# Layer 0's gate columns on TensorE in the scan, layer 1's mix columns behind layer 0's experts, longer runs in layer 1's experts, and the second mixer's norms by halves

## The chip, the core and the metric

The kernel runs on one core of one Trainium2 chip. A core has TensorE (PE, matrix products), VectorE (DVE), ScalarE (ACT), GpSimd (POOL) and SyncE (SP), each with its own queue of instructions that it executes in order, and 16 DMA engines that move data between the chip's large memory and the core's own. The metric is the device time of one execution, in microseconds (us).

## The reference, cut to what matters

One call runs two layers of one model and then a block of another on 512 latent tokens of width 1024 (layer 0 also on 256 context tokens):

```
for i in (0, 1):
    mod_l = split(silu(c) @ ada_w[i] + ada_b[i], 6)        # six vectors of 1024; mod_c alike from c_ctx
    h = rmsnorm(x, norm_mix_g[i]) * (1 + mod[1]) + mod[0]
    x = x + mod[2] * mixer_i(h)                            # mLSTM, then retention
    h = rmsnorm(x, norm_ffn_g[i]) * (1 + mod[4]) + mod[3]
    x = x + mod[5] * expert_choice_ffn(h)                  # 16 experts, each takes its top tokens
x = rmsnorm(x, final_norm_g)
hn = rms_norm(x, attn_norm_g_2); proj = hn @ w_in_2        # then attention, GLA, pooling, ffn
```

An expert computes silu(xs @ w_gate) * (xs @ w_up), times w_down, for its 64 latent (32 context) tokens; the results are added back to the tokens' rows with the gate as weight.

## The kernel before, in words

The stages follow each other on TensorE: norms and the qk dense of the mLSTM (to about 120 us), its v dense (to 208), its sigmoid gate dense (to 293), the scan (to 410), out-projection and routing (to 540), layer 0's experts (to 1101), retention (to 1404), out-projection and routing (to 1486), layer 1's experts (to 1964), and the second block with its mixer and ffn (to the end).

**Dense products** are exact splits: each fp32 matrix is a high and a low part (whi, wlo; hhi, hlo), and three matmuls (L295 to L297) make one product, a triple. Into these runs, `fill(n)` puts steps of waiting generators, n steps per triple: 2 means two steps after each triple, 0.25 one in four. What is left at a dense's end is emptied by `fill(1000)`.

**Modulation columns.** `ada_chunk` (L165 and around) computes one of the six vectors of a layer for both c and c_ctx: VectorE multiplies 1024 x 1024 weights by silu(c) into ada_v, 16 instructions, two for each of eight row blocks; TensorE sums over the partitions with 16 f32 matmuls in 32 records (L170); a gate vector (2, 5) goes to memory as `modd`, the others become columns. Chunks 2 to 5 of layer 0 are the generators of the sigmoid gate dense, each of six steps. `ada_mix` (L205 to L233) computes vectors 0 and 1 of layer 1 on TensorE instead: eight loads of 1 MB, 32 matmuls (64 records, L217), a copy on ScalarE (L221), four transposes, and three VectorE instructions. It is the generator of the scan, where `fill(2)` (L685) takes two steps at a time. The generator of the v dense is `mlstm_gates` (tiles pc, L541 to L583), 54 steps.

**Layer 0's experts.** `expert_stream` hands out a ring of 20 weight slots in a fixed order: four of the stream's own (w), wb0, ot, whb, whp, wb1. `st.get()` gives the next loaded slot, `st.done()` issues the load of the next chunk into the slot that has come free; a chunk is 1 MB, eight f32 records of 512 columns in the latent form (L879). TensorE's order is written out by hand (`pinned`). At the end of the last expert its two results are multiplied by the gates (yl, yc, L1157) and scattered into xl and xc by GpSimd (L1158); seven warming matmuls (L114) run on yl; all pools of the stage are closed; the retention loads its tokens from xl and xc into rt_x (L1524), norms them (L361), transposes them (L1533) and starts its first dense.

**Layer 1's experts** take 64 tokens each, and the groups of tokens lie ready for two experts at a time. Odd experts (and expert 0) *gather* for the next pair: eight gathers of eight records each (L1306; tile tp, three buffers), evicted by ScalarE and VectorE in turn (L1310, L1308) into xT, then `facts` (L1318). Two gathers lie ahead of the transposes of hl (L1392), two behind them, and one after each quarter of the down product (tile dl). Even experts add the results of the pair before: `combine` makes eight sums (tile cb, two buffers, L1345 and L1346), each followed by a VectorE addition into X (L1348). The first stands in the up product (tile pl) after its first quarter, then one per quarter, one behind it, two after hl = silu * up (L1385), two after the transposes. `split` (L1325 to L1331) prepares the results for the sums in two halves of 64 rows, b = 0 then 1; for odd experts (sw = 1) half b is put at place b ^ 1, and the sums read place 0 first. The last eight sums stand alone at the stage's end.

**Second mixer** (L1829 and on): for each of four token tiles, ScalarE squares and sums x (L1829), VectorE (tiles 0 and 3) or GpSimd (1 and 2) multiplies by the final norm's weight (L1830), ScalarE squares again (L1831), two reciprocal roots follow (`rstd`, L100 and L102; a root needs a table load on ScalarE when another function was there before), VectorE makes the normed tile (L1842), TensorE transposes it (L1770), and the first dense runs a tile behind (L295 to L297). For tile 0 TensorE is kept warm with small matmuls (L114) on the results of the chain.

## Time and profile before

| | us |
|---|---|
| median of 3 runs | 2591.66 (2591.22 to 2591.9) |
| the profiled execution | 2597.43 |
| its span | 2595.6 |
| TensorE busy in it | 2488.7 |
| VectorE busy | 1078.6 |
| ScalarE busy | 699.0 |
| GpSimd busy | 555.1 |
| mean granted clock of TensorE | 0.977 |

The span is the time between the first and the last recorded instruction. Busy is the time in which an engine works on an instruction; a matmul of TensorE appears as a row (PE) beside its weight load (PEld), and rows of one run overlap, so a run is measured from start to start. The granted clock is 1.0 at 2.4 GHz and 0.5 at 1.2 GHz. A row in order of time has its start, its duration, engine, line, operation, the written tile <- the read ones, their count, and in brackets the idle time before it with what ended it. SPq rows are issues of DMAs. A row of a stretch (window) has its start and end, its length, the busy us of PE, PEld, DVE, ACT and POOL with the instructions of each, the granted clock, the DMA engines' mean share and the GB/s that they moved.

### The profile page before, as it was taken

To read this page: it belongs to the slowest core of one execution; us is meant where nothing else is said; L and a number is where in the kernel's file an instruction comes from. 1 tells how busy PE (TensorE), PEld (TensorE's weight loads), DVE (VectorE), ACT (ScalarE), POOL (GpSimd) and SP (SyncE) were. 2 spreads that over 40 slices of the span, in tenths; PEclk is the share of its full clock that TensorE was granted. 3 is DMA by queue.
4 is the path that set the end of the run, shared out by engine and by line. 5 is a ranking of instruction groups with operands and counts; after the bars stand their busy time and mean duration, and the time that the engine had idled before them with its cause. 6 is when DMAs were issued, how large, how long until landed. Compare 5 with 4: busy or idle time off the path is not lost. (4 is left out here: it accounts for less than half of the span.)

```text
span 2595.6 us, 36637 instructions
## 1 busy us (share of the span) xinstructions
PE 2488.7 (96%) x15126; PEld 1621.3 (62%) x15126; DVE 1078.6 (42%) x2105; ACT 699.0 (27%) x1351; POOL 555.1 (21%) x339
## 2 busy tenths in 40 slices
PE   7999898989999999999999999999997999999999
PEld 6777586844444333378777754444446766788887
DVE  5578687341111111153666332222225558433310
ACT  4332365421111111044224311111114436322211
POOL 2213325311111110124456200000001221122233
PEclk9999999989999999999999999999998999999999
DMA  7215603379999999632464599999992221233431
GB/s 256 81 51 199 240 34 133 136 289 340 395 393 389 399 398 409 246 116 72 160 230 158 215 373 407 419 420 420 419 394 82 83 87 32 64 95 96 121 105 57
DMA packets 145273, 584.79 MB, mean 225 GB/s; under 512 B 17671, under 2 KB 47535, under 8 KB 93908
## 3 DMA queue, kind: packets, MB, share of 16 engines
q1 hardware_dynamic: 138684, 569.87, 57.4%
q0 software_dynamic: 6416, 12.59, 2.2%
q8 instruction: 119, 1.95, 0.3%
q14 instruction: 46, 0.38, 0.0%
q10 hardware_dynamic: 8, 0.01, 0.0%
HBM read 567.70 MB, written 14.71 MB: 224 GB/s over the span
## 5 line engine op out<-in xcount | busy, mean ns | idle before, releaser
L277 POOL TENSOR_TENSOR wlo<-w,whi 128x1024 fp32r<-128x1024 f32 x103 | 269.3, 2617 | 1103.5 <-ACT whi L276 616.7
L879 PE MATMUL pl<-w,xT 128*64 128x512 f32 x1240 | 287.5, 595 | 0.0
L276 ACT ACTIVATE whi<-w 128x1024 fp32r<-128x1024 f32 x148 | 154.4, 1050 | 457.2 <-PE acc L297 188.9
L295 PE MATMUL acc<-whi,hhi 128*128 128x512 f32 (+2 forms) x672 | 267.8, 399 | 1.1 <-ACT pre L446 1.1
L296 PE MATMUL acc<-wlo,hhi 128*128 128x512 f32 (+2 forms) x672 | 263.7, 392 | 2.3 <-POOL wlo L277 2.3
L297 PE MATMUL acc<-whi,hlo 128*128 128x512 f32 (+2 forms) x672 | 262.2, 391 | 0.0
L297 PE MATMUL acc<-hhi,wlo 128*128 128x512 f32 (+2 forms) x528 | 198.8, 377 | 3.2 <-POOL wlo L277 3.2
L295 PE MATMUL acc<-hhi,whi 128*128 128x512 f32 (+2 forms) x528 | 198.8, 377 | 2.9 <-DVE hlo L290 1.5
L296 PE MATMUL acc<-hlo,whi 128*128 128x512 f32 (+2 forms) x528 | 199.2, 378 | 0.6 <-POOL hlo L407 0.5
L879 PEld LDWEIGHTS pl<-w,xT 128*64 128x64 f32 x1240 | 102.9, 137 | 152.5 <-issue 131.9
L277 DVE TENSOR_TENSOR wlo<-w,whi 128x1024 fp32r<-128x1024 f32 (+2 forms) x45 | 59.6, 1324 | 254.6 <-ACT whi L276 254.4
L879 PE MATMUL pl<-wb,xT 128*64 128x512 f32 x640 | 152.1, 596 | 0.0
L295 PEld LDWEIGHTS acc<-whi,hhi 128*128 128x128 f32 x672 | 128.8, 192 | 30.7 <-issue 6.1
L296 PEld LDWEIGHTS acc<-wlo,hhi 128*128 128x128 f32 x672 | 129.1, 192 | 28.3 <-POOL wlo L277 3.8
L297 PEld LDWEIGHTS acc<-whi,hlo 128*128 128x128 f32 x672 | 128.7, 192 | 26.0 <-issue 2.4
L165 DVE SCALAR_TENSOR_TENSOR ada_v<-w,csil,ada_v 128x1024 f32<-128x1024 f32 x84 | 133.0, 1619 | 8.1 <-DMA w<-in_ada_w_dram 6.8
L297 PEld LDWEIGHTS acc<-hhi,wlo 128*128 128x128 f32 (+1 forms) x528 | 98.4, 187 | 22.8 <-POOL wlo L277 3.4
L295 PEld LDWEIGHTS acc<-hhi,whi 128*128 128x128 f32 (+1 forms) x528 | 98.3, 186 | 22.4 <-DVE hlo L290 1.7
L296 PEld LDWEIGHTS acc<-hlo,whi 128*128 128x128 f32 (+1 forms) x528 | 98.5, 187 | 19.7 <-POOL hlo L407 0.7
L879 PEld LDWEIGHTS pl<-wb,xT 128*64 128x64 f32 x640 | 51.3, 137 | 80.0 <-issue 72.2
L1306 PEld LDWEIGHTS tp<-sh,rt_y 128*128 128x128 f32 x576 | 68.2, 191 | 34.6 <-issue 33.3
L1048 ACT ACTIVATE xT<-ro_tp,cols,ffnA 128x32 f32<-128x32 f32 x128 | 41.3, 375 | 159.0 <-DVE xT L1045 152.5
(599 smaller groups left out, 4176.0 us busy)
## 6 DMA issues: line engine op xcount, KB each, us to landing
w<-in_moe_w_gate_dram SPq DMA_DIRECT2D x91, 1024.0 KB, 19.8
w<-in_moe_w_down_dram SPq DMA_DIRECT2D x84, 1024.0 KB, 16.5
w<-in_moe_w_up_dram SPq DMA_DIRECT2D x68, 1024.0 KB, 21.6
wb<-in_moe_w_up_dram SPq DMA_DIRECT2D x53, 1024.0 KB, 13.9
w<-in_ada_w_dram SPq DMA_DIRECT2D x40, 1024.0 KB, 5.9
wb<-in_moe_w_down_dram SPq DMA_DIRECT2D x38, 1024.0 KB, 22.6
wb<-in_moe_w_gate_dram SPq DMA_DIRECT2D x30, 1024.0 KB, 20.0
w<-in_ret_w_in_dram SPq DMA_DIRECT2D x16, 1024.0 KB, 5.5
```

What stands on the lines that cost most here:

```text
L165: nc.vector.scalar_tensor_tensor(acc[r], w[:, kk], x, acc[r], ALU.mult, ALU.add)
L276: nc.scalar.activation(hi, raw[:, k:k + n, :], AF.Copy)
L277: (nc.vector if fast and (k // n) % 2 == 0 else nc.gpsimd).tensor_sub(lo, raw[:, k:k + n, :], hi.bitcast(F32))
L295: nc.tensor.matmul(out, lh[0], rh[0], start=start, stop=False)
L296: nc.tensor.matmul(out, lh[0], rh[1], start=False, stop=False)
L297: nc.tensor.matmul(out, lh[1], rh[0], start=False, stop=stop)
L879: self.pinned(self.nc.tensor.matmul(out[64 * b:64 * b + 64, :], lat(kk), w[:, kk - k0, 512 * c:512 * c + 512], start=kk == 0, stop=kk == K ...
L1048: nc.scalar.activation(xT[:, kk, a:b], tp[:, k, a:b], AF.Identity, scale=A[:, kk, 1:2], bias=B[:, kk, 1:2])
L1306: pin(nc.tensor.matmul(tp, y[:, t, 128 * k:128 * k + 128], oh[:, t, 0:m], start=t == 0, stop=t == 3))
```

## The change

It has seven parts. (1) The generators of layer 0's sigmoid gate dense are only chunks 3 and 4, one step in eight triples instead of one in four. (2) The v dense takes 0.7 steps of `mlstm_gates` per triple instead of 2 (the limit in `dense_tok` goes from 1 to 0.5 only so that this dense splits its weights as before). (3) Vectors 2 and 5 of layer 0 are computed by `ada_gates` on TensorE in the scan, in the places that `ada_mix` had: loads in halves, a bias that is added by one VectorE instruction, four stores to `modd`. (4) `ada_mix` moves to the end of layer 0's experts: its eight loads are the last chunks of the ring, its matmuls stand in TensorE's order behind the last down product, and the seven warming matmuls are gone. (5) In layer 1's experts, six gathers and the facts stand in a run behind the transposes and ahead of the down product; the sums of a pair stand two at a time (after the first and the third quarter of the up product; two after hl; two after the transposes). (6) In `split` the half that the sums read first is made first, and ahead of the last expert ScalarE does one square root of a constant. (7) In the second mixer, squares, products and the normed tile are made by halves of 512 columns; the second norm's mean is worked out as mean(g^2 x^2) + EPS (mean(x^2) + EPS), so that one root gives the factor; the other root is taken behind it; tile 0's steps have a higher priority in the scheduler.

```diff
+import contextlib
 import math
...
-    def ada_mix(self):
+    def ada_gates(self):
...
         nc, I = self.nc, self.I
-        gcol = self.ap.tile([128, KD], F32, name="ada_g")
-        nc.sync.dma_start(gcol, I["norm_mix_gT"][:, 1, :])
-        bias = self.ap.tile([128, 2, KD], F32, name="ada_b")
-        nc.sync.dma_start(bias, I["ada_bT"][:, 6:8, :])
+        bias = self.ap.tile([128, 512], F32, name="ada_gb")
+        parts = [(q, D * j + 512 * b) for q, (j, b) in enumerate(((2, 0), (2, 1), (5, 0), (5, 1)))]
+        for q, o in parts:
+            nc.sync.dma_start(bias[32 * q:32 * q + 32, :], I["ada_b"][0, o:o + 512].partition_broadcast(32))
         ps = self.aps.tile([128, 512], F32, name="ada_acc")
...
             w = self.wslot()
-            nc.sync.dma_start(w, I["ada_w"][1, 128 * k:128 * k + 128, 0:2 * D])
+            for c, j in enumerate((2, 5)):
+                nc.sync.dma_start(w[:, D * c:D * c + D], I["ada_w"][0, 128 * k:128 * k + 128, D * j:D * j + D])
             for q in range(4):
...
             yield
-        ms = self.ap.tile([128, 512], F32, name="ada_ms")
+        nc.vector.tensor_add(bias, bias, ps)
+        for q, o in parts:
+            nc.sync.dma_start(self.modd[0][:, o:o + 512], bias[32 * q:32 * q + 2, :])
+        yield
+    def ada_mix(self, get, done, pool, psum):
+        nc, I = self.nc, self.I
+        gcol = pool.tile([128, KD], F32, name="ada_g", bufs=1)
+        nc.sync.dma_start(gcol, I["norm_mix_gT"][:, 1, :])
+        bias = pool.tile([128, 2, KD], F32, name="ada_b", bufs=1)
+        nc.sync.dma_start(bias, I["ada_bT"][:, 6:8, :])
+        sc = pool.tile([128, KD, 32], F32, name="ada_sc", bufs=1)
+        nc.vector.memset(sc, 0.0)
+        nc.vector.tensor_copy(sc[:, :, 0:2], self.csil.rearrange("p r k -> p k r"))
+        ps = psum()
+        for k in range(KD):
+            w = get()
+            for q in range(4):
+                self.pinned(nc.tensor.matmul(ps[32 * q:32 * q + 32, :], sc[:, k, :], w[:, 512 * q:512 * q + 512],
+                                             start=k == 0, stop=k == KD - 1))
+            done()
+        ms = pool.tile([128, 512], F32, name="hl")
         nc.scalar.copy(ms, ps)
-        tp = self.aps.tile([128, 512], F32, name="ada_acc")
+        tp = psum()
         for b in range(4):
...
                                        gcol[:, :, None].to_broadcast([128, KD, 2]), ALU.add, ALU.mult)
-        yield
...
             src = wsrc[128 * k0:128 * (k0 + kn), n0:n0 + nn].rearrange("(k p) n -> p k n", p=128)
-            for k1, n, whi, wlo in self.split_weights(self.load_weights(src), hp, k0 == 0 and not 0 < fill < 1):
+            for k1, n, whi, wlo in self.split_weights(self.load_weights(src), hp, k0 == 0 and not 0 < fill < 0.5):
                 for k in range(n):
...
                                v[:, t, 4 * half:4 * half + 4, 0:128],
-                               ps.rearrange("p (h d) -> p h d", h=4), AF.Copy, scale=0.125), fill=2)
+                               ps.rearrange("p (h d) -> p h d", h=4), AF.Copy, scale=0.125), fill=0.7)
         self.fill(1000)
...
         acc = lambda: self.aps.tile([128, 512], F32, name="ada_acc")
-        self.fillers = [self.ada_chunk(0, j, 2, avp, acc) for j in (2, 3, 4, 5)]
+        self.fillers = [self.ada_chunk(0, j, 2, avp, acc) for j in (3, 4)]
         rp = self.pool("ml_o", side="right")
...
                            lambda t, ps, half=half: nc.scalar.activation(
-                               sigo[:, t, 512 * half:512 * half + 512], ps, AF.Sigmoid), fill=0.25)
+                               sigo[:, t, 512 * half:512 * half + 512], ps, AF.Sigmoid), fill=0.125)
         self.fill(1000)
         avp.close()
-        self.fillers = [self.ada_mix()]
+        self.fillers = [self.ada_gates()]
         whp.close()
...
         nc, I = self.nc, self.I
-        chunks = ((e, w, k) for e, w in order for k in range(0, KD, 2))
+        chunks = ((e, w, k) for e, w in order for k in range(0, KD, 1 if w == "mix" else 2))
         ring, ready = [], []
...
             e, w, k = c
-            t = slot().rearrange("p (k n) -> p k n", k=2)
+            t = slot()
+            if w == "mix":
+                nc.sync.dma_start(t, I["ada_w"][1, 128 * k:128 * k + 128, 0:2 * D])
+                ready.append(t)
+                return
+            t = t.rearrange("p (k n) -> p k n", k=2)
             if behind is not None:
...
             order += [(e, "gate"), (e - 1, "down"), (e, "up")]
-        st = self.expert_stream(i, order + [(E - 1, "down")])
+        st = self.expert_stream(i, order + [(E - 1, "down"), (None, "mix")])
         st.open(self.wslot, self.NW)
...
                                          in_=y, in_offset=None, compute_op=ALU.add)
-            return y
-        last = []
...
                              lambda k: hTc[:, k % 2, 32 * (k // 2):32 * (k // 2) + 32], dl, dc,
-                             (lambda: last.append(scatter(e, 0, dl)), lambda: scatter(e, 1, dc)))
+                             (lambda: scatter(e, 0, dl), lambda: scatter(e, 1, dc)))
             if e + 1 < E:
                 product(1, e + 1, between=lambda: xTs.update({e + 2: turn(xg, new())}) if e + 2 < E else None)
+        self.ada_mix(st.get, st.done, wk, tile)
         self.pin = False
-        yl = last[-1]
-        self.warm(ps.tile([128, 512], F32, name="pl0"), yl, 7)
         ps.close()
...
             pin(nc.vector.scalar_tensor_tensor(y, dl, gi[:, e, 0:1], m5[:, sw, :], ALU.mult, ALU.mult))
-            for b in range(2):
+            for b in (sw, 1 - sw):
                 s = slice(64 * b, 64 * b + 64)
...
             pl = [ps.tile([128, 512], F32, name="pl", bufs=2) for _ in range(2)]
+            if e == E - 1:
+                self.tc.keep_in_program_order(nc.scalar.activation(wk.tile([128, 1], F32, name="ro_sq", bufs=1), self.epsc,
+                                                                   AF.Sqrt))
             lat = lambda k: xT[:, k, e - e0, :]
...
                 steps(work, 1)
-            self.expert_gemm(st, lat, None, pl[1], None, late=lambda k: steps(work, 1 if k else 0))
-            steps(work, 1)
+            self.expert_gemm(st, lat, None, pl[1], None, late=lambda k: steps(work, 2 if k in (2, 6) else 0))
             pin(nc.vector.tensor_tensor(hl, hl, pl[1], ALU.mult))
...
             if e in groups:
-                gather(oh, *groups[e], range(2, 4))
+                gather(oh, *groups[e], range(2, KD))
+                facts(oh, *groups[e])
             dl = ps.tile([128, 512], F32, name="dl")
             sw = e % 2
-            self.expert_gemm(st, lambda k: hTl[:, k % 4, 64 * (k // 4):64 * (k // 4) + 64], None, dl, None, swap=sw,
-                             late=lambda k: gather(oh, *groups[e], (3 + k // 2,)) if e in groups and k else None)
+            self.expert_gemm(st, lambda k: hTl[:, k % 4, 64 * (k // 4):64 * (k // 4) + 64], None, dl, None, swap=sw)
             if e in groups:
-                gather(oh, *groups[e], (KD - 1,))
-                facts(oh, *groups[e])
                 e0 = groups[e][0]
...
                     nc.vector.tensor_copy(glt[:, t, :], acc[:, 256:272])
+        def norms(t, x):
+            ss = xp.tile([128, 4], F32, name="s_ss")
+            sq = xp.tile([128, D], F32, name="s_sq")
+            for b in range(2):
+                s = slice(512 * b, 512 * b + 512)
+                nc.scalar.activation(sq[:, s], x[:, s], AF.Square, accum_out=ss[:, b:b + 1])
+                (nc.gpsimd if t % 3 else nc.vector).tensor_mul(x[:, s], x[:, s], gf[:, s])
+                nc.scalar.activation(sq[:, s], x[:, s], AF.Square, accum_out=ss[:, 2 + b:3 + b])
+            m = xp.tile([128, 4], F32, name="s_m")
+            nc.vector.tensor_scalar(m[:, 0:1], ss[:, 0:1], 1.0 / D, EPS, ALU.mult, ALU.add)
+            nc.vector.scalar_tensor_tensor(m[:, 0:1], ss[:, 1:2], 1.0 / D, m[:, 0:1], ALU.mult, ALU.add)
+            nc.vector.tensor_scalar(m[:, 1:2], ss[:, 2:3], 1.0 / D, None, ALU.mult)
+            nc.vector.scalar_tensor_tensor(m[:, 1:2], m[:, 0:1], EPS, m[:, 1:2], ALU.mult, ALU.add)
+            r2 = m[:, 2:3]
+            nc.scalar.activation(r2, ss[:, 3:4], AF.Sqrt, scale=1.0 / D, bias=m[:, 1:2])
+            nc.vector.reciprocal(r2, r2)
+            if t == 0:
+                w = psum.tile([128, 512], F32, name="acc", tag="acc")
+                self.warm(w, ss[:, 2:3], 6)
+                self.warm(w, r2, 3)
+            for b in range(2):
+                s = slice(512 * b, 512 * b + 512)
+                nc.vector.scalar_tensor_tensor(sq[:, s], x[:, s], r2, ga[:, s], ALU.mult, ALU.mult)
+            return sq, m
         for t in range(NT):
             x = X[:, t, :]
-            ss = xp.tile([128, 2], F32, name="s_ss")
-            sq = xp.tile([128, D], F32, name="s_sq")
-            nc.scalar.activation(sq, x, AF.Square, accum_out=ss[:, 0:1])
-            (nc.gpsimd if t % 3 else nc.vector).tensor_mul(x, x, gf)
-            nc.scalar.activation(sq, x, AF.Square, accum_out=ss[:, 1:2])
-            r = r1[:, t:t + 1]
-            nc.vector.tensor_copy(r, self.rstd(xp, ss[:, 0:1], 1, D))
-            nc.vector.tensor_scalar(ss[:, 1:2], ss[:, 1:2], r, r, ALU.mult, ALU.mult)
-            r2 = self.rstd(xp, ss[:, 1:2], 1, D)
-            nc.vector.tensor_mul(r2, r2, r)
-            if t == 0:
-                w = psum.tile([128, 512], F32, name="acc", tag="acc")
-                self.warm(w, r, 6)
-                self.warm(w, r2, 3)
-            nc.vector.scalar_tensor_tensor(sq, x, r2, ga, ALU.mult, ALU.mult)
+            with self.tc.high_priority() if t == 0 else contextlib.nullcontext():
+                sq, m = norms(t, x)
+            nc.scalar.activation(m[:, 3:4], m[:, 0:1], AF.Sqrt)
+            nc.vector.reciprocal(r1[:, t:t + 1], m[:, 3:4])
             self.tile_T(sq, hhi, hlo, t, pst, 2)
...
```

## Rows read from the trace of the kernel before

**Rows 1.** The page's part 1: busy us, share of the span, instructions.

```profile
PE 2488.7 (96%) x15126; PEld 1621.3 (62%) x15126; DVE 1078.6 (42%) x2105; ACT 699.0 (27%) x1351; POOL 555.1 (21%) x339
```

**Rows 2.** Windows of four stretches: us from the start, busy us by engine, clock.

```profile
169.80:173.20 3.40, 3.40 (x12) 2.56 (x11) 0.00 (x0) 0.72 (x1) 0.00 (x0) 0.51 0.00 0
250.00:275.00 25.00, 21.10 (x94) 15.48 (x93) 24.96 (x22) 2.71 (x3) 7.28 (x3) 0.86 0.67 235
1115.30:1118.70 3.40, 3.40 (x11) 2.56 (x10) 2.03 (x8) 1.94 (x6) 0.00 (x0) 0.50 1.06 394
1700.00:1800.00 100.00, 99.68 (x558) 48.84 (x554) 24.66 (x53) 12.83 (x23) 0.00 (x0) 1.00 1.01 420
```

**Rows 3.** Waits of TensorE, 208.5 to 293: us in total, times, longest.

```profile
PE ada_acc L170 <- DVE ada_v L165: 5.9, 3, 3.9
```

**Rows 4.** Order of time, end of layer 0's experts: start, duration, engine, line.

```profile
1098.51 2.77 PE L886 MATMUL ro_lg<-w,hT 128*32 128x256 f32 x48
1101.21 6.28 PE L114 MATMUL pl<-yl,cs 128*128 128x512 f32 x14
1103.77 2.01 SPq L1524 DMA_DIRECT2D rt_x<-xl  x4
1114.80 0.47 PE L295 MATMUL acc<-whi,hhi 128*128 128x512 f32 x1
```

**Rows 5.** Order of time, last Silu to second mixer: ScalarE, VectorE, TensorE.

```profile
1941.50 0.60 ACT L1371 ACTIVATE hl<-pl 128x512 f32<-128x512 f32 x1 [4.80 <-PE pl L879]
1968.71 1.06 ACT L1829 ACTIVATE s_sq<-X 128x1024 f32<-128x1024 f32 x1 [5.76 <-DVE X L1348]
1969.87 1.28 ACT L100 ACT_TABLE_LOAD   x1
1971.17 0.29 ACT L100 ACTIVATE rs_t<-s_ss,epsc 128x1 f32<-128x1 f32 x1
...
1974.36 1.66 DVE L1830 TENSOR_TENSOR X<-X,s_gf 128x1024 f32<-128x1024 f32 x1
...
1980.41 1.91 PE L1770 MATMUL tT_tp<-cs,s_sq 128*128 128x128 f32 x8
```

**Rows 6.** Lines on VectorE, 185 to 293: instructions, busy us, mean ns.

```profile
L165 DVE SCALAR_TENSOR_TENSOR ada_v<-w,csil,ada_v 128x1024 f32<-128x1024 f32 x56 | 85.8, 1586 | 7.2 <-DMA w<-in_ada_w_dram 6.8
```

**Rows 7.** Lines on TensorE, 208.5 to 293.

```profile
L170 PE MATMUL ada_acc<-ada_v,cs 128*32 128x256 f32 x64 | 5.8, 450 | 5.9 <-DVE ada_v L165 5.9
```

**Rows 8.** Order of time on TensorE in the scan, 292 to 330.

```profile
314.20 1.92 PE L217 MATMUL ada_acc<-w,ada_sc 128*32 128x512 f32 x14
```

**Rows 9.** Order of time on TensorE, an odd expert of layer 1.

```profile
1591.58 7.04 PE L879 MATMUL pl<-wb,xT 128*64 128x512 f32 x32
1598.55 2.05 PE L1306 MATMUL tp<-sh,rt_y 128*128 128x128 f32 x16
...
1600.87 1.95 PE L1306 MATMUL tp<-sh,rt_y 128*128 128x128 f32 x16
1602.75 1.94 PE L879 MATMUL dl<-w,hTl 128*64 128x512 f32 x8
1604.62 1.16 PE L1306 MATMUL tp<-sh,rt_y 128*128 128x128 f32 x8
1605.71 1.94 PE L879 MATMUL dl<-w,hTl 128*64 128x512 f32 x8
```

**Rows 10.** Order of time on TensorE, the even expert before it.

```profile
1566.26 0.50 PE L1345 MATMUL cb<-Yhi,sh 128*128 128x512 f32 x1
...
1573.83 0.50 PE L1345 MATMUL cb<-Yhi,sh 128*128 128x512 f32 x1
...
1574.40 0.39 PE L1345 MATMUL cb<-Yhi,sh 128*128 128x512 f32 x1
...
1575.94 0.66 PE L1392 MATMUL tp<-cs,hl 128*128 128x128 f32 x4
```

**Rows 11.** The page's part 6: DMA issues, count, KB each, us to landing.

```profile
w<-in_moe_w_gate_dram SPq DMA_DIRECT2D x91, 1024.0 KB, 19.8
```

## The prediction, made before the changed kernel ran

> **What bounds the kernel now.** I read the engines' shares first, then stretches of time stage by stage, then the waits and order of instructions where the change works. TensorE is busy 2488.7 us, 96% of the span of 2595.6 [rows 1], so nearly every us of TensorE's own order is a us of the end, and the rest is 107 us of waits plus the price of the stretches at half speed. Three places matter here. In the last dense of layer 0's first mixer (the sigmoid gate, about 208 to 293 us) VectorE is full, 24.96 of 25.00 us, TensorE works 21.10 and its clock averages 0.86 [rows 2]: the modulation chunks on VectorE set the pace, and TensorE waits 5.9 us for them [rows 3]. In layer 1's experts TensorE never stands for long and the DMA engines are at share 1.01 with 420 GB/s [rows 2]: two limits lie close together. Around the ends of both expert stages TensorE waits for a chain of small steps [rows 4, 5].
>
> The profiled execution took 2597.43 us, 1.83 over its span and 5.77 over the median 2591.66. I sum against 2597.43 and take 5.77 off at the end.
>
> **1. Two of four chunks leave VectorE beside the sigmoid gate.** A chunk is 16 multiply-adds; four take 85.8 us in 56 of them, eight plain products come on top [rows 6], so two chunks less free 47 us of an engine that is full. Three things follow: the wait of 5.9 us goes [rows 3]; the clock of 0.86 over 25 us means 7.0 us at half speed, where TensorE was partly waiting, so 2.8 of the 3.5 us at stake; and half of the chunks' 64 matmuls goes, 5.8 us busy [rows 7], 2.9 by the busy time and 2.0 as I take it, since records of busy time overlap. Sum **-10.7**. From above 12.3 at most; from below 2, if the two chunks that remain are still late. At one step in eight triples (before: one in four) the first remaining chunk is wanted about 27 us after the dense's start and the second about 60, and each needs some 24 us of VectorE: I expect no wait.
>
> **2. The gates of the scan spread over the v dense (0.7 steps a triple, not 2).** 54 steps now lie on 27 triples, then on 77. One of the dense places runs at 0.51 of the clock from 169.8 for 3.4 us [rows 2]; with its continuation and a like one from 145.9 that is 10.2 us, so 5.1 to gain if all go. Against it, 27 more breaks of the run of matmuls, at 0.13 us for each break as in the experts (step 5): +3.5. I take **-2**, bounds -5.1 and +3.5.
>
> **3. The gate columns on TensorE in the scan.** They take the places of the layer 1 mix: the same 64 records (14 of them busy 1.92 us [rows 8]) at the same eight places. Instead of four transposes and a copy there is one VectorE sum of 512 columns (under 1 us: the product of 1024 takes 1.66 [rows 5]), and SP issues 16 loads of half the size, four bias loads and four stores. What lies behind these on SP's queue is wanted only after the scan. **0**, bounds -2 and +3.
>
> **4. The mix at the end of layer 0's experts.** Now the last weights of the experts end at 1101.21, seven warming matmuls fill 6.28 us until the scattered sums are back, the loads of rt_x are issued at 1103.77 and the first matmul of the retention starts at 1114.80, 11.03 us later [rows 4]. The mix takes the place of the warming: 64 records of 512 columns. 48 records of 256 columns take 2.70 us, 1098.51 to 1101.21 [rows 4], so 64 of twice the width take 7.2 us, and by the scan's runs, 1.92 for 14, up to 8.8 [rows 8]. It ends at 1108.4 to 1110.0. Its time is hidden in the wait, but its weights are not: eight more loads pass through the ring of 20 slots, the last three into wb1, and after the pools are closed rt_x lies on this memory. So the loads of rt_x have to wait for the last matmul of the mix, 4.7 to 6.2 us later than now, and all that follows with them. TensorE then stands idle longer; the retention starts at half speed already (0.50 from 1115.3 [rows 2]), and I add one more such stretch, 1.7. **+6.4**; bounds 0, if rt_x lies elsewhere, and 9.6, with two such stretches and the longer time for the mix. The eight loads themselves come when the ring is otherwise done; cover as in step 6.
>
> **5. Six gathers in a run, a pair's sums two at a time.** In an odd expert, a run of 32 records of the experts' products takes 6.97 us, from 1591.58 to 1598.55, or 1.74 for eight; cut up, eight take 1.87, 1602.75 to 1604.62. Sixteen records of the gather take 1.88, 1600.87 to 1602.75, or 0.94 for eight; alone eight take 1.09 [rows 9]. Four pieces of either kind are joined: 4 x (0.13 + 0.15) = 1.12, and with eight groups **-9.0**. The cover is the evictions, by ScalarE and VectorE in turn into three buffers: if they don't keep up with a gather each 0.94 us, half goes (-5); -10.5 at best. In an even expert, from the first sum at 1566.26 to the transposes at 1575.94 are 9.68 us with six sums and 24 records of products; a sum behind another takes 0.57, 1573.83 to 1574.40 [rows 10]. Six at 0.57 and 24 records in two runs, 3 x 1.74 + 2 x 0.13, are 8.90; 0.78 saved by seven pairs is **-5.5**, bounds -7 and -3 (the sums are still held by VectorE's additions, two buffers).
>
> **6. The weights behind it.** Fourteen us less in this stage is 3%. A load of 1 MB at 420 GB/s takes 2.50 us, and 192 of them are as long as the stage; with 20 slots a slot comes round in some 50 us, of which a load takes 19.8 from issue to landing [rows 2, 11], leaving some 30. 14.5 us fit in it: 0 here, and a rival below.
>
> **7. Square root ahead of the last Silu.** It costs table loads, 1.28 us each [rows 5], two of them with a root of 0.29 in between: 2.85 us in the 4.80 us for which ScalarE is idle ahead of that Silu [rows 5]. It saves nothing that I can see, since Silu's own load comes after it and the second mixer's root needs its load again. **0**, bounds 0 and +2. The Trainium skill (ScalarE: Activation LUTs, "Table sets: the hidden batching unit" and "What ACT_TABLE_LOAD costs") says to batch activations by set and counts about 2.66 us for each switch, drain included; this speaks against the edit. By an estimate from that figure two switches take 5.3 us, 0.5 more than the idle time, and the sum would be -24.8. The trace has the load at 1.28 and the next activation right behind it at 1971.17, so the drain isn't seen here.
>
> **8. The second mixer's norms by halves, tile 0 first; the split's half that is wanted first.** Tile 0 is complete at 1968.7, where its first square starts, and its transposes begin at 1980.41 [rows 5], 11.7 us later; meanwhile VectorE does the sums of the other tiles first. With priority: a square and its read-out take 1.16 whole (1968.71 to 1969.87), so about 0.7 for a half; two products of a half 0.83 each (half of 1.66), the last square 0.7, the table load 1.28, the root 0.29, and about 0.85 for the reciprocal and half of the last product: 5.5, so 1974.2; with three of VectorE's additions between, at most 0.83 each by the same row, 1976.7. That is 4 to 6 us earlier. The next tile isn't earlier by as much, but tile 0's matmuls last 6 us. If priority does nothing, the product starts where it does now, 1974.36, and two halves, 0.7, 0.29 and 0.85 end at 1977.9: 2.5 earlier. More and smaller instructions on three engines for tiles 1 to 3: +2 at worst. **-4.5**, bounds -8 (two half-speed stretches gone as well) and +2.
>
> **Sum.** -10.7 - 2 + 0 + 6.4 - 9.0 - 5.5 + 0 + 0 - 4.5 = -25.3: 2572.1 for a profiled execution, 2566.4 for the median.
>
> **Rivals.** (a) Layer 1's experts become bound by the DMA: for it speak share 1.01 and 420 GB/s [rows 2], against it the 30 us of cover. Half of the 14.5 us is lost: 2573.7. Chance 0.12. (b) The change beside the sigmoid gate doesn't do what it says, because a chunk left over is late all the same: only 2 of 10.7 are gained, 2575.1. For it: VectorE also splits the weights there. Against: 47 us freed. Chance 0.10. (c) rt_x doesn't wait for the mix: step 4 is 0, 2560.0. For it: the planner may place it otherwise. Chance 0.08. (d) The table loads land on the path: the root stands right ahead of the Silu on ScalarE, and if ScalarE comes to it only when the Silu's input is there, both loads and the root, 2.85 us, lie ahead of the Silu [rows 5]: 2569.3. For it: nothing but that order fixes its place. Against: its input is long there, and ScalarE is idle for 4.80 us. Chance 0.04. The rule of the Trainium skill named in step 7 is the one that this would bear out. (e) Slower: TensorE runs out of weights in layer 1's experts and its clock falls with it. The place is the second half of that stage; it decides itself where the cover of 30 us is used up. Then the 14.5 us are lost, and each of the last eight experts brings a stretch of 6.8 us at half speed as at the retention's start, 3.4 lost each, 27 us: 2566.4 + 14.5 + 27 = 2607.9. Against: the clock is 1.00 there now [rows 2] with the DMA as full. Chance 0.04. The forecast has the remaining 0.62.
>
> **Range.** All bounds at once would be 2547 and 2602; errors of eight terms rarely add up, the rivals (a) to (d) lie between 2560 and 2575, and the half-speed stretches, 1.7 us for each 3.4, can shift by four either way. **2551 to 2583** holds 8 in 10. About 0.2% (5.2 us) is what a measurement of this kernel can tell from no change: faster 0.93 (forecast, (a) to (d), less a little for several misses together), same 0.03, slower 0.04.
>
> **What would show it.** Right: no TensorE wait for ada_v and a clock of 1.0 between 225 and 285; rt_x's loads issued right after the last mix matmul, some 5 us later against the last expert; odd experts shorter by 1.1 us and even ones by 0.8 with no wait for tp; no wait for w in layer 1's experts; transposes of the second mixer some 5 us closer to the last product. The forecast is wrong if one of the two large gains (1 and 5) isn't there, or if the retention's start slips by more than 10 us.

## The result and the profile after

| | before | after |
|---|---|---|
| median, us | 2591.78 (4 runs, 2591.22 to 2593.78) | 2564.54 (4 runs, 2557.19 to 2569.42) |
| profiled execution | 2597.43 | 2557.19 |
| its span, mean granted clock | 2595.6, 0.977 | 2555.4, 0.986 |

The ratio is 0.9891, 95% interval 0.9874 to 0.9909: 27.2 us faster, where 25.3 had been forecast, and 2564.5 where 2566.4. The two profiled executions lie 40.2 us apart, more than the medians. By their mean clocks TensorE ran at half speed for 119 us of the one and 72 us of the other ((1 - 0.977) x 2595.6 / 0.5 and alike); if half of such a stretch is lost, 24 us of the 40 are the clock's. The four executions of the changed kernel, 2557.19, 2564.32, 2564.76 and 2569.42, had clocks of 0.986, 0.981, 0.983 and 0.979. So single stages are compared below with those of the experiments too, since each of these leaves most stages as they are. Stages are taken from start to start of TensorE's rows:

| stage, us | before | after | experiments that leave it alone | forecast |
|---|---|---|---|---|
| v and sigmoid gate dense (first triple to the scan's first rb) | 174.1 | 156.6 | 156.6 to 158.2 | -12.7 |
| scan | 127.1 | 124.5 | 126.6 to 129.7 | 0 |
| out-projection, routing | 120.0 | 116.9 | 115.4 to 120.1 | 0 |
| layer 0's experts, to their last row | 560.1 | 558.7 | 557.2 to 560.3 | 0 |
| from there to the retention's scan (rt_U) | 111.5 | 118.9 | 118.5 to 118.8 | +6.4 |
| rest of the retention, routing | 273.3 | 273.9 | 270.9 to 276.8 | 0 |
| layer 1's experts (first gather to last product) | 471.3 | 457.0 | 456.5 to 457.5 | -14.5 |
| from there to the second mixer's scan (g) | 102.0 | 96.6 | 96.5 to 98.9 | -4.5 |
| rest | 532.4 | 531.7 | 528.5 to 533.2 | 0 |

The page of after has TensorE as full as [rows 1] has it, with 38.1 us less of busy time:

```profile
PE 2450.6 (96%) x15144; PEld 1625.4 (64%) x15144; DVE 1027.4 (40%) x2084; ACT 701.5 (27%) x1370; POOL 554.9 (22%) x341
```

Windows (columns as in [rows 2]): the v dense and the sigmoid gate dense, before and then after, each from its first triple.

```profile
119.53:211.88 92.35, 89.20 (x413) 67.82 (x412) 76.45 (x100) 30.34 (x49) 21.82 (x7) 0.94 0.26 84
211.88:293.66 81.78, 75.91 (x363) 57.03 (x362) 68.38 (x51) 17.61 (x25) 20.11 (x7) 0.96 0.61 218
116.78:204.20 87.42, 85.33 (x413) 65.81 (x412) 63.19 (x91) 29.66 (x49) 19.46 (x7) 0.98 0.19 61
204.20:273.36 69.16, 68.91 (x330) 55.51 (x328) 36.09 (x27) 17.56 (x24) 19.96 (x7) 1.00 0.50 167
```

The sigmoid gate dense is 12.6 us shorter and takes 69.2 in every kernel with two chunks. The v dense is 4.9 us shorter; it had 10.2 us at half speed, now 3.4. In five of the experiments that leave it alone it has 6.8 and takes 89 us, so it gained 3.3 to 4.9. Three stretches of after, beside the sigmoid gate, at the retention's start and in layer 1's experts:

```profile
230.00:255.00 25.00, 25.00 (x124) 19.96 (x124) 20.60 (x13) 7.47 (x10) 8.08 (x3) 1.00 0.59 191
1085.60:1095.80 10.20, 4.79 (x21) 4.21 (x21) 7.45 (x10) 8.78 (x16) 5.53 (x2) 0.50 1.03 402
1660.00:1760.00 100.00, 100.00 (x574) 53.57 (x572) 26.15 (x54) 11.60 (x22) 0.00 (x0) 1.00 1.01 419
```

Beside the sigmoid gate TensorE is busy without a gap at full clock where [rows 2] has 21.10 of 25 us at 0.86; VectorE has 20.60 of 25. No wait for ada_v ([rows 3]) is left. In layer 1's experts the DMA engines are as full as before.

The end of layer 0's experts in order of time, after; it answers to [rows 4]:

```profile
1073.61 4.47 PE L242 MATMUL ro_tp<-w,ada_sc 128*32 128x512 f32 x40
1077.90 2.76 PE L242 MATMUL ro_tp<-wb,ada_sc 128*32 128x512 f32 x24
...
1080.72 1.76 SPq L1552 DMA_DIRECT2D rt_x<-xl  x4
...
1090.78 3.33 PE L115 MATMUL acc<-rs_r,cs 128*128 128x128 f32 x14 [8.76 <-DVE rs_r L103]
...
1095.72 0.53 PE L319 MATMUL acc<-whi,hhi 128*128 128x512 f32 x1
```

The mix (L242) starts where the warming was, 7.0 us long. rt_x's loads are issued at 1080.72, as it ends, 7.1 us behind the last expert's end (before: 2.56). Then TensorE waits 8.76 us, and the retention's first dense product comes 22.1 us behind the last expert's end instead of 13.6. SP's waits say why the loads are late:

```profile
SPq L1470 <- PE ro_tp L242: 21.5, 1, 21.5
SPq L1552 <- PE ro_tp L242: 1.1, 1, 1.1
```

The rope table's load (L1470) waits for the mix for 21.5 us, and behind it on SP stand two of the retention's weight loads and rt_x (L1552), which waits another 1.1.

An odd expert and an even one of layer 1, after; they answer to [rows 9] and [rows 10]:

```profile
1575.45 2.05 PE L1333 MATMUL tp<-sh,rt_y 128*128 128x128 f32 x16
...
1577.77 5.52 PE L1333 MATMUL tp<-sh,rt_y 128*128 128x128 f32 x48
1583.23 1.23 PE L1345 MATMUL tp<-mo_at,sh 128*64 128x2 f32 x29
...
1584.49 7.06 PE L909 MATMUL dl<-w,hTl 128*64 128x512 f32 x31
```

```profile
1544.20 0.50 PE L1372 MATMUL cb<-Yhi,sh 128*128 128x512 f32 x1
...
1545.33 3.65 PE L909 MATMUL pl<-w,xT 128*64 128x512 f32 x16
1548.91 0.50 PE L1372 MATMUL cb<-Yhi,sh 128*128 128x512 f32 x1
...
1550.04 1.94 PE L909 MATMUL pl<-w,xT 128*64 128x512 f32 x8
...
1552.94 0.60 PE L1422 MATMUL tp<-cs,hl 128*128 128x128 f32 x4
```

Six gathers take 5.46 us in a run (1577.77 to 1583.23), 0.91 each, with no wait for tp. From the first sum to the transposes there are 8.74 us, before 9.68. But the last expert, in the same view, has gaps that nothing before it has:

```profile
1904.16 1.94 PE L909 MATMUL pl<-wb,xT 128*64 128x512 f32 x8 [0.32 <-DMA wb<-in_moe_w_up_dram]
1906.56 1.94 PE L909 MATMUL pl<-wb,xT 128*64 128x512 f32 x8 [0.46 <-DMA wb<-in_moe_w_up_dram]
1909.04 1.94 PE L909 MATMUL pl<-wb,xT 128*64 128x512 f32 x8 [0.54 <-DMA wb<-in_moe_w_up_dram]
1911.52 1.94 PE L909 MATMUL pl<-wb,xT 128*64 128x512 f32 x8 [0.55 <-DMA wb<-in_moe_w_up_dram]
...
1921.83 1.94 PE L909 MATMUL dl<-w,hTl 128*64 128x512 f32 x8 [0.67 <-DMA w<-in_moe_w_down_dram]
```

Four quarters of the up product and one of the down product wait for their weights, 2.5 us in all. How early the weights lay ready before the change can be read from the same place there: the issue of the last down product's four loads, their size and median time to landing, and the product.

```profile
1912.80 7.81 SPq L833 DMA_DIRECT2D w<-in_moe_w_down_dram  x4
w<-in_moe_w_down_dram SPq DMA_DIRECT2D x4, 1024.0 KB, 20.3
1950.51 7.09 PE L879 MATMUL dl<-w,hTl 128*64 128x512 f32 x32 [0.68 <-ACT hTl L1393]
```

The first of them is there at 1933.1 and used at 1950.51: 17.4 us of cover at the end of the stage, not the 30 of the prediction.

From the last Silu to the second mixer, after, on ScalarE, VectorE and TensorE; it answers to [rows 5]:

```profile
1899.11 1.28 ACT L1393 ACT_TABLE_LOAD   x1
1900.40 0.20 ACT L1393 ACTIVATE ro_sq<-epsc 128x1 f32<-128x1 f32 x1
1900.62 1.28 ACT L1402 ACT_TABLE_LOAD   x1
1903.88 0.60 ACT L1402 ACTIVATE hl<-pl 128x512 f32<-128x512 f32 x1 [1.98 <-PE pl L909]
...
1931.00 0.63 ACT L1861 ACTIVATE s_sq<-X 128x512 f32<-128x512 f32 x1 [1.29 <-DVE X L1375]
...
1936.34 1.28 ACT L1886 ACT_TABLE_LOAD   x1
...
1937.74 0.28 ACT L1871 ACTIVATE s_m<-s_ss,s_m 128x1 f32<-128x1 f32 x1
...
1931.49 2.21 DVE L301 TENSOR_TENSOR wlo<-w,whi 128x1024 fp32r<-128x1024 f32 x1
1933.62 1.28 DVE L1862 TENSOR_TENSOR X<-X,s_gf 128x512 f32<-128x512 f32 x2
...
1939.48 0.16 DVE L1872 RECIPROCAL s_m<-s_m 128x1 f32<-128x1 f32 x1
...
1940.14 1.66 DVE L1879 SCALAR_TENSOR_TENSOR s_sq<-X,s_m,s_ga 128x512 f32<-128x512 f32 x2
...
1942.46 1.03 PE L1798 MATMUL tT_tp<-cs,s_sq 128*128 128x128 f32 x8
```

The two table loads lie in ScalarE's idle time; it still waits 1.98 us for the Silu's input. Tile 0's first square is at 1931.00, its transposes at 1942.46: 11.5 us, as before (11.7). Its steps stand behind others: a weight split of 2.21 us on VectorE (1931.49) ahead of its products, the other root's table load at 1936.34, and a reciprocal that VectorE does at 1939.48, 1.5 us behind the root.

### The profile page after: what moved, and what is told of

Its sections match the earlier page's. It is cut to its first block, busy times and chain, and to the rows that moved or that the text cites. A ratio compares the mean times of both kernels' runs of the same rounds, so it can differ in the third digit from the quotient of the medians.

```text
span 2555.4 us, 36703 instructions
## 1 busy us (share of the span) xinstructions
PE 2450.6 (96%) x15144; PEld 1625.4 (64%) x15144; DVE 1027.4 (40%) x2084; ACT 701.5 (27%) x1370; POOL 554.9 (22%) x341
## 5 line engine op out<-in xcount | busy, mean ns | idle before, releaser
L166 DVE SCALAR_TENSOR_TENSOR ada_v<-w,csil,ada_v 128x1024 f32<-128x1024 f32 x56 | 91.9, 1663 | 10.6 <-DMA w<-in_ada_w_dram 9.5
L909 PE MATMUL dl<-w,hTl 128*64 128x512 f32 x352 | 81.0, 597 | 1.3 <-ACT hTl L1423 0.7
```

The source lines that it names most:

```text
L166: nc.vector.scalar_tensor_tensor(acc[r], w[:, kk], x, acc[r], ALU.mult, ALU.add)
L909: self.pinned(self.nc.tensor.matmul(out[64 * b:64 * b + 64, :], lat(kk), w[:, kk - k0, 512 * c:512 * c + 512], start=kk == 0, stop=kk == K ...
```

## The experiments

All are the changed kernel with one thing different; times beside those of the changed kernel (2564.54) are medians, and since its own runs spread over 12 us, a stage in the profile says more than they do.

**The gates spread over the v dense, taken back.**

```diff
-    ..., AF.Copy, scale=0.125), fill=0.7)
+    ..., AF.Copy, scale=0.125), fill=2)
```

> The changed kernel with the v dense at two steps of the scan's gates per triple, as before the change. Theory of the prediction: the dense is longer by 2 us (5.1 us of half speed back, 3.5 us fewer breaks). Rival from the profile after: the v dense became 7.0 us shorter, so all of this comes back, 6 to 8 us, with half-speed stretches near 146 and 170 and a wait for tile pc.

The two dense products took 160.0 us, 1.8 to 3.4 more than with the spread, all of it in the v dense (90.9 us with 6.8 at half speed; 89 with the spread and as much half speed); median 2570.27. So the 2 us of the theory are right. The 7.0 us of the rival are counted from the first pc, which the spread puts three triples later; from its first triple the v dense had become 4.9 shorter. The wait for pc is back, most of the 1.8:

```profile
PE pc L603 <- DVE dg L596: 1.7, 1, 1.7
```

**The chunks back beside the sigmoid gate, nothing in the scan.**

```diff
-    for j in (3, 4)]
+    for j in (2, 3, 4, 5)]
...
-    ..., AF.Sigmoid), fill=0.125)
+    ..., AF.Sigmoid), fill=0.25)
...
-    self.fillers = [self.ada_gates()]
+    self.fillers = []
```

> The changed kernel with chunks 2 to 5 of layer 0 on VectorE beside the sigmoid gate again, at one step in four triples, and nothing in the scan's places (the mix stays at the end of layer 0's experts). Theory: the sigmoid gate dense is 10 to 13 us longer again, with 5 to 6 us of waits for ada_v and a half-speed stretch; the scan without its 64 records is shorter by up to 8 us, their time there being partly hidden. Rival (the sigmoid gate dense gained only its two chunks' matmuls): 2 to 4 us.

174.3 us for the two dense products, 16.0 to 17.7 more, over the range that was expected, and as long as before; the scan took 120.1 in the one profile, 4.4 to 9.6 less. Median 2572.85. The waits and a window of this kernel, and VectorE's last multiply-adds for the chunks, before and here:

```profile
PE ada_acc L171 <- DVE ada_v L166: 9.9, 3, 4.7
260.00:285.00 25.00, 20.31 (x104) 15.24 (x105) 24.76 (x20) 2.70 (x3) 5.13 (x2) 0.98 0.67 239
272.52 14.19 DVE L165 SCALAR_TENSOR_TENSOR ada_v<-w,csil,ada_v 128x1024 f32<-128x1024 f32 x10
271.47 13.36 DVE L166 SCALAR_TENSOR_TENSOR ada_v<-w,csil,ada_v 128x1024 f32<-128x1024 f32 x11
```

TensorE waits 9.9 us, not 5.9, has 10.2 us at half speed, not 6.8, and works 20.31 of 25 us beside a VectorE that is full. The v dense keeps what the spread gave it (87.4 us), and the sigmoid gate dense loses as much (86.8, before 81.8). VectorE is done with the four chunks at 284.8 here and at 286.7 before, though TensorE begins this dense at 205.0 here and at 211.9 before, and the dense can't end ahead of its last chunk. So each of the two changes is worth more with the other one made: 174.1 before, 160.0 with the chunks alone, 174.3 with the spread alone, 156.6 to 158.2 with both.

**The gathers, the sums, and the weights behind them.**

```diff
-                gather(oh, *groups[e], range(2, KD))
-                facts(oh, *groups[e])
+                gather(oh, *groups[e], range(2, 4))
...
+                             late=lambda k: gather(oh, *groups[e], (3 + k // 2,)) if e in groups and k else None)
+            if e in groups:
+                gather(oh, *groups[e], (KD - 1,))
+                facts(oh, *groups[e])
```

> The changed kernel with the gathers of layer 1's experts as before: two ahead of and two behind the transposes, then one behind each quarter of the down product, the facts last. Theory: each of seven odd experts 1.12 us longer, experts' stage 8 to 9.5 us longer. Rival (the weights' loads set the pace of the stage): under 4 us.

```diff
-    late=lambda k: steps(work, 2 if k in (2, 6) else 0))
+    late=lambda k: steps(work, 1 if k else 0))
+    steps(work, 1)
```

> The changed kernel with the sums of a pair as before, one behind each quarter of the up product. Theory: each of seven even experts 0.78 us longer, experts' stage 5 to 6 us longer. Rival (the weights' loads set the pace): under 2 us.

Layer 1's experts took 464.0 us without the run of gathers and 460.5 without the pairs of sums, 7.0 and 3.5 more than 457.0; medians 2572.98 and 2573.29. Both are less than forecast, and their sum, 10.5, is less than the 14.3 between before and after. From one expert's transposes to the next but one's, a pair takes 58.28 us before, 57.24 with the sums alone, 56.91 with the gathers alone, and 55.86 after: 1.37 for the gathers and 1.04 for the sums, more than forecast (1.12 and 0.78), and they add up. The difference is at the end: from the last but one expert's transposes to the last one's are 23.4 to 23.5 us in before and in both experiments, and 26.2 after. So the weights are asked:

```diff
+            if i and w == "gate" and 4 <= e < 14:
+                nc.sync.dma_start(t[:, :, 0:512], I["moe_w_" + w][i, e, k // 2][:, :, 0:512])
```

> The changed kernel with only half of the gate weights of experts 4 to 13 of layer 1 loaded, 20 MB less (their gate products use the half that is there twice; the same matmuls run). Theory (at the end of layer 1's experts the weights come too late, since the stage's DMA is full): from the last but one to the last expert's transposes 23.4 to 23.6 us instead of 26.2, no wait for wb in the last up product, all other experts as they are; the stage 2.5 to 3 us shorter. Rival (the last expert's waits have another cause, such as SP's order or the tail's loads): 25.5 us or more.

In its one execution the last interval took 23.43 us, the stage 453.2, 3.8 less, and all other pairs 55.86 as in after. The last expert in order of time, with the up product in one piece:

```profile
1906.05 7.04 PE L914 MATMUL pl<-wb,xT 128*64 128x512 f32 x32
1913.95 0.66 PE L1427 MATMUL tp<-cs,hl 128*128 128x128 f32 x4 [0.86 <-DVE hl L1420]
```

So the DMA engines set the end of the stage after the change, and with 20 MB less they don't.

**The price of the mix at the end of layer 0's experts.** First its weights were put elsewhere in the ring:

```diff
+            last = chunks[-20:]
+            plain, mix = last[:12], last[12:]
+            chunks = chunks[:-20] + [(mix if s in (3, 7, 8, 13, 14, 15, 16, 17) else plain).pop(0) for s in range(20)]
```

> The changed kernel, with the eight mix loads put into ring slots whose memory the retention's first tiles don't use (slots 3, 7, 8 and 13 to 17 instead of 12 to 19); the last down product's weights take the slots under rt_x, as before the change. TensorE's order is untouched. Theory (the start of the retention is late because rt_x, and the loads queued on SP behind the rope table, wait for the mix matmuls on memory that they share): the rt_x loads are issued some 2.6 us after the last down product again instead of 7.1, they land in some 4 us instead of 8, and the first dense product of the retention comes 13 to 15 us after the last context product instead of 22.1: 7 to 11 us less than the changed kernel. Rival (the mix's own 7 us and the longer idle time make the delay): the distance stays at 19 us or more, 3 us gained at most.

Neither theory could be told: rt_x's loads still waited for the mix, though none of its weights lies under rt_x any more. They go out at 1090.26, right behind the mix's last records (on wb, the one mix slot of the pool wb1, to 1090.20), and the rope table's at 1089.40, right behind those on w (slots of whp, to 1089.35): a tile waits for all tiles of a closed pool that its own memory follows. The first dense product came 20.6 us behind the last expert's end, which is in the range of the rival but not for its reason; the scan 117.1, 1.8 earlier; median 2564.64. So with other slots, and the rope table's load behind rt_x's:

```diff
-    ... if s in (3, 7, 8, 13, 14, 15, 16, 17) else plain ...
+    ... if s in (3, 7, 8, 12, 13, 14, 15, 16) else plain ...
...
+        nc.sync.dma_start(rope, self.I["rope"])      # behind rt_x's loads
```

> The changed kernel with the mix loads in ring slots 3, 7, 8 and 12 to 16, of which none lies in the pools wb0 and wb1 that rt_x follows, and with the rope table's load issued behind rt_x's loads. In the last attempt rt_x still waited for the mix, since a tile waits for all tiles of a closed pool that it follows, not for those bytes alone. Theory (the wait for the memory delays the retention): rt_x's loads are issued some 2.6 us after the last expert product, land some 4 us later, and the first dense product of the retention comes 14 to 16 us after the last context product, not 22.1 as in the changed kernel: 6 to 8 us less by this stage. Rival (the mix's time and its chain on ScalarE and VectorE make the delay, or the weight splits, which still wait for the mix): 19 us or more.

Its start of the retention in order of time:

```profile
1087.96 1.04 PE L242 MATMUL ro_tp<-w,ada_sc 128*32 128x512 f32 x8
...
1090.78 1.84 SPq L1563 DMA_DIRECT2D rt_x<-xl  x4
...
1098.46 3.90 ACT L300 ACTIVATE whi<-w 128x1024 fp32r<-128x1024 f32 x4
...
1104.69 2.64 DVE L388 TENSOR_SCALAR rt_x<-rt_x,rs_r 128x1024 f32<-128x1024 f32 x1
...
1107.39 0.69 PE L1573 MATMUL rt_tp<-cs,rt_x 128*128 128x128 f32 x2 [3.89 <-DVE rt_x L388]
...
1109.05 0.76 PE L319 MATMUL acc<-whi,hhi 128*128 128x512 f32 x1
```

rt_x's loads go out 2.8 us behind the last expert's end and the first square starts at 1095.34, as the theory says, and yet the first dense product comes 21.1 us behind it. The gain has become another wait: the weight splits still come behind the mix (with the first slots one of them waited for the mix by itself, to 1089.46; here ScalarE does them behind the mix's copy), and at 1098.46 four of them stand on ScalarE, 3.90 us, ahead of the second tile's square, and VectorE's part of them makes the second tile's product late (1104.69 to 1107.3); the transposes wait 3.89 us for it. To the scan it is 119.3. Median 2568.32. At last the mix went ahead of the last down product, where its memory is free in time for all of these, and the warming back to its place:

```diff
-        st = self.expert_stream(i, order + [(E - 1, "down"), (None, "mix")])
+        st = self.expert_stream(i, order + [(None, "mix"), (E - 1, "down")])
...
+            if e == E - 1:
+                self.ada_mix(st.get, st.done, wk, tile)
...
-        self.ada_mix(st.get, st.done, wk, tile)
+        self.warm(ps.tile([128, 512], F32, name="pl0"), last[-1], 7)
```

> The changed kernel with the layer 1 mix ahead of the last expert's down product instead of behind it, and the seven warming matmuls behind that product again. The mix's 7 us then stand on TensorE's path, but no tile of the retention waits for them: neither rt_x's loads nor the weight splits. Theory (the price at the retention's start is the wait of all its tiles for the mix): 13 to 15 us from the last context product to the retention's first dense product again, not 22.1; from the last expert's hidden product to the retention's first scan step 7 us of mix come in and 7 to 9 go out, and a shorter stretch at half speed, so 0 to 4 us less than the changed kernel in this stage. Rival (the order doesn't matter, 7 us are 7 us): 0, within 1 us.

```profile
1086.78 2.77 PE L916 MATMUL ro_lg<-wb,hT 128*32 128x256 f32 x48
...
1093.03 1.76 SPq L1556 DMA_DIRECT2D rt_x<-xl  x4
...
1103.32 0.47 PE L319 MATMUL acc<-whi,hhi 128*128 128x512 f32 x1
```

The first dense product comes 13.8 us behind the last expert's end (1089.48) and the scan 110.9; the experts took 565.2, 6.5 more. Together 676.1 us against 677.6 after and 671.6 before. So the delay is that of tiles that wait for the mix, and putting it on the path costs nearly the same. Median 2565.39 in five runs, no better than the changed kernel.

**The second mixer.** Four parts were taken back alone: the order of split's halves, the norms by halves, the priority of tile 0, and the square root ahead of the last Silu.

```diff
-            for b in (sw, 1 - sw):
+            for b in range(2):
```

> The changed kernel with the halves of split in the old order (b = 0, then 1, for odd experts too). Theory from the last pair in the profile after: the last sums start 5.0 us behind the last product, two at once, where before it was 6.1 and 8.8; so undoing it costs 2.5 to 4 us from the last product to the second mixer's first transposes. Rival (the prediction counted the order as under 1 us and the norms as the rest): under 1 us.

```diff
-            with self.tc.high_priority() if t == 0 else contextlib.nullcontext():
-                sq, m = norms(t, x)
+            nc.scalar.activation(sq, x, AF.Square, accum_out=ss[:, 0:1])
...
```

> The changed kernel with the second mixer's norms as before (whole tiles, two roots in the chain, no priority for tile 0). Theory: from the last sum to the first transposes of the second mixer 7 us again instead of 3.5, so 3 to 5 us longer. Rival (the gain came from the order of the split, not from the norms): under 1 us.

```diff
-            with self.tc.high_priority() if t == 0 else contextlib.nullcontext():
+            with contextlib.nullcontext():
```

> The changed kernel without the higher priority for tile 0 of the second mixer's norms. The prediction's step: with the priority tile 0's transposes come 4 to 6 us earlier than before, without it 2.5; so 1.5 to 3.5 us longer here. Rival from the profile after (tile 0's chain takes 11.5 us from its first square to its transposes, as before, since VectorE's weight split and additions stand between its steps all the same): within 1 us.

```diff
-            if e == E - 1:
-                self.tc.keep_in_program_order(nc.scalar.activation(..., self.epsc, AF.Sqrt))
```

> The changed kernel without the square root ahead of the last Silu. Theory: no difference (under 0.5 us at the last Silu and in the second mixer's chain), since its two table loads fit into ScalarE's idle time and the second mixer's load is needed in either case. Rival (the loads delay the last Silu): 0.5 to 2.9 us shorter.

| from the last product, us | 1st sum | 8th sum | transposes | scan (g) | at half speed near it |
|---|---|---|---|---|---|
| before | 6.7 | 16.0 | 23.4 | 102.0 | 17.0 |
| after | 5.5 | 15.5 | 19.3 | 96.6 | 10.2 |
| after with another clock (in the kernel with half the weights) | 5.5 | 15.4 | 21.3 | 98.5 | 17.1 |
| old split order | 6.7 | 17.0 | 22.5 | 99.7 | 17.1 |
| old norms | 5.5 | 14.2 | 20.6 | 98.7 | 13.6 |
| no priority | 5.5 | 13.3 | 20.1 | 97.8 | 10.2 |
| no square root | 5.5 | 15.1 | 19.3 | 96.5 | 10.2 |

The unchanged part comes at two times, 96.5 and 98.5 to 98.9, by where the half speed falls, so each is compared with its like. The old order costs 1.2 us, which sits between the two theories. The old norms, with half speed between the two, cost 0 to 2.2 to the scan, less than the 3 to 5 expected: from the 8th sum to the transposes it is 6.4 us again instead of 3.8 (5.9 with the other clock), but the 8th sum is 1.3 earlier. The lacking priority costs 0.8 to the transposes and 1.2 to the scan: without it the sums end 2.2 us earlier, because VectorE's additions no longer stand behind tile 0's steps, and tile 0 is later by about as much. The square root makes no difference. Medians 2569.38, 2568.40, 2566.83 and 2566.15.

## Why the prediction was right, step by step

**Step 1**: 10.7 forecast, 12.6 measured in the sigmoid gate dense, a little over the bound of 12.3. The mechanism was right (no wait, full clock). The wait gave its 5.9 us, the 6.8 us at half speed 3.4 instead of 2.8, and what is left for the two chunks' matmuls and their breaks is 3.3, not 2.0. (A chunk has 8 matmuls in 16 records, not the 16 in 32 named above; the 64 of the four were counted rightly.) Rival (b) falls.

**Step 2**: 2 forecast, 3.3 to 4.9 measured, inside its bounds; 1.8 to 3.4 when taken back alone. Of the 10.2 us at half speed 3.4 or 6.8 stay, and the 27 more breaks at 0.13 us were not to be seen: at like half speed the v dense is 1.8 us shorter, about the wait for pc (1.7). What the sum of the two steps left out is that the second has no worth without the first: while VectorE has four chunks to do, their end sets the end, and both together gave 15.9 to 17.6 where 12.7 was forecast.

**Step 3**, nothing: the scan is 124.5 to 129.7 in all kernels with the same 64 records, 127.1 before. The 64 records are not free there, though: without them it is 120.1 (one profile).

**Step 4**: 6.4 forecast, 7.0 to 7.4 measured. The wait was placed rightly (rt_x behind the mix, 4.55 us later against the last expert), but its price was put together wrongly. Rope table and weights wait as well. rt_x's first square starts 8.2 us behind the issue instead of 4.2, with two loads of weights ahead of rt_x's and their splits ahead of the square on ScalarE; that the shared loading makes the difference was not tried. rt_x alone set free gains 1 us at the first product and nothing at the scan. Half speed lasted 10.2 us there (3.4 before), not the 6.8 that I had counted. Rival (c) falls: rt_x does lie behind the mix.

**Step 5**: 1.12 and 0.78 forecast, 1.37 and 1.04 measured, 18 us for all groups instead of 14.5. A gather in a run takes 0.91, less than the 0.94 of two, and the sum that waited 0.32 for VectorE's addition no longer does.

**Step 6** was wrong. Its 30 us came from the ring's round and the median landing, as if the cover were the same all along. But a load takes 2.50 us, and TensorE takes one in 2.43 before (58.28 for the 24 of a pair) and in 2.33 after, so the cover shrinks through the stage: before the change it was 17.4 us at the end. With 18 us off the stage the last expert waits 2.5 us for its weights, and 3.8 us come back when 20 MB less are loaded. This is rival (a) at half its size (of (e) nothing is seen, the clock stays at 1.00 there), and it hid that step 5 was too small: 14.3 us remained of 18, where 14.5 stood in the forecast. That the stage came out within 0.2 us is luck, two misses that cancel.

**Step 7**: nothing, as forecast, by the trace and by taking it away. ScalarE had both loads and the root done in 2.79 us (1899.11 to 1901.90), 1.98 us ahead of the Silu's input; rival (d) falls with it. By an estimate from the Trainium skill's figure for a switch with its drain, about 2.66 us (ScalarE: Activation LUTs, "What ACT_TABLE_LOAD costs"), the Silu would have come some 0.7 us late. No row here has a drain: the root starts at 1900.40, right behind the 1.28 us of the load.

**Step 8**: 4.5 forecast, 3.1 to 5.5 measured, for other reasons, so the number was met by luck. Tile 0's own chain did not get shorter, 11.5 us (13.5 with the other clock) for 11.7: I had counted its steps one behind the other, with three additions between, and left out the weight split, the other root and its table load, and that VectorE's small steps queue behind additions that wait for TensorE at half speed. The whole is earlier because the sums start 1.2 us earlier and tile 0 is complete 7.8 us behind the last product, not 11.7 (11.1 with the old split order, which had no term in the sum); the order is worth 1.2 us at the scan, the priority about 1. What part of the rest belongs to the clock can't be told by these runs.

**The sum.** -12.7 became -15.9 to -17.6, +6.4 became +7.0 to +7.4, -14.5 became -14.3 and -4.5 became -3.1 to -5.5: some 26 to 30 by the stages, 27.2 by the medians, 25.3 forecast. The total was nearer than its parts: steps 1, 2 and 5 were too small, step 6 took back what step 5 gave too much, and the clock moves the profiles by as much as the difference.

## What to carry to other kernels

Before moving work into a wait, ask what memory it holds to its end: everything that is allocated over the closed pools waits, not the one load that one has in mind, and freeing that one load shows the next. When a stage has two limits close together, sum a gain only up to the second one, and look for the loss in the stage's last part: read the cover there, from landing to use, and not from means over the stage. A gain ahead of a stage that a full helper engine paces is waited off, so it isn't additive: take the changes back one by one and both together. And when a change moves the row at which a stage is cut, cut it at another one: three triples were 2 us here.

## What the runs showed of the hardware that was not expected

The granted clock differs from run to run in the same kernel (0.979 to 0.986 in four executions of the changed one, 12.2 us of time), and so do the places of half speed: the same rows from the last product to the second mixer's scan take 96.5 or 98.5 us with 10.2 or 17.1 us at half speed, and those of the v dense 87.4 or 89 with 3.4 or 6.8. These two stages are known to 2 us only.
